# RWKV-7 time mixing on one core: up projections over the whole array, and two groups of per-head sums issued as one

## The chip, the core and the metric

The kernel runs on one core of a Trainium2 chip. Five compute queues matter here: TensorE (PE in the profile; its weight loads are PEld), VectorE (DVE), ScalarE (ACT), GpSimd (POOL), and SyncE (SP), which issues nearly all transfers. The metric is the device time of one execution, in microseconds (us).

## What is computed

One layer: RMS norm, RWKV-7 time mixing with a gate, output projection, residual. SEQ is 2048 and D_MODEL 1024: 16 heads of 64. The part that the change touches, from the reference:

```python
w_lo = jnp.tanh(x_w @ w_in[:, c[4]:c[5]])
a_lo = x_a @ w_in[:, c[5]:c[6]]
w_raw = (w0 + w_lo @ w_up).astype(f32)
log_decay = -jnp.exp(-jax.nn.softplus(-w_raw) - 0.5)
a = jax.nn.sigmoid((a0 + a_lo @ a_up).astype(f32))
...
kk = heads(k * k_k)
kk = kk / jnp.maximum(jnp.sqrt(jnp.sum(kk * kk, axis=-1, keepdims=True)), 1e-12)
...
y = y + jnp.sum(r_h * k_h * r_k.astype(f32), axis=-1, keepdims=True) * v_h
```

`w_up` and `a_up` take 64 low-rank values of a token to 1024 channels: these are the up projections. The sum of `kk * kk` over a head's 64 channels is the sum of squares; the sum of `r * k * r_k` over them is the bonus.

## The kernel before

**Stages.** First (to about 487 us) come the low-rank, value and gate projections of all tokens. Then the tokens go in eight blocks of 256 (NB of TB): for blocks 0 to 6 a function `step(b, p)` runs for p = 0 to 7, one pair of heads each, with 128 channels on the partitions (about 505 to 1054 us). The last block's steps are interleaved with the first chunks of the recurrence, which then runs to the end beside the output projection.

**Numbers in two parts.** A projection's operands are split into a high part and a low part, and a product is three matmuls: high by high, high by low, low by high. A projection of a pair is 24 matmuls of 128x128 by 128x256. The up projections are split otherwise: `up` (L785) holds the weights of both, [:, 0] for the decay and [:, 1] for a, with the high part in one half of the 128 rows and the low part in the other. `split_lo` (L773) makes `lo`, in which the high part of the 64 low-rank values stands twice, in both halves, in [:, 0] and [:, 1]; their low part stands in one half of [:, 2] for the decay and in the other for a. `chain_a` (L789) then issues two matmuls over all 128 rows (L801), and two over 64 rows for the low part (L803). The result `wa` goes to ScalarE (th, ta).

**A step.** `step(b, p)` does four things: r projection of its pair (`rps`, L851), k projection of a pair of the next block (`kps`, L545, begun at the step's start and copied and squared by ScalarE within it: k and sq), products of the pair (`mps`, L887, masked into `mo` by VectorE; `tps`, transposes, L872), and the up projection and decays of the pair after (`chain_a`). `rb` (L829) spreads the factors of the keys' norms over the rows.

**Sums.** `sums` (L712) takes the sums over heads of two pairs at once, by a matmul with a 128x32 matrix of ones and zeros (`hsel`). Each pair has its own 32 of the 128 columns of the array, given by `tile_position`, so a tile of PSUM has the sums of eight pairs in four column tiles of two. The sums of squares of the next block go to `ssp` (from sq), in steps 0, 2, 4 and 6, behind the transposes. The bonuses of this block go to `bnp` (from u, which VectorE makes from the r projection and k): in steps 2, 4 and 6 those of pairs p - 2 and p - 1, behind the masked products; the last two pairs come in step 0 of the next block by `bn_save` (L757), ahead of the up projection. `save` (L718) copies a finished tile to SBUF: `bnc`, `ssc`.

**What sets the order.** The instructions of TensorE, VectorE, ScalarE and GpSimd run in the order in which the code issues them (L1040, a manual schedule). A scheduler places the transfers in SyncE's queue. Each engine works through its queue in order: whatever waits holds all that stands behind it.

**Buffers.** `up` has two buffers, so the weights of a pair are loaded two steps ahead (`load_up(p + 2)`).

Of the kernel before, what the change touches and what calls it, by code (L numbers as in the profile page):

```python
# [39 lines left out]
def rwkv7_kernel(ctx, tc, a, T):  # L40
# [48 lines left out]
    # W_out's rows in the place of two blocks' mixes, once those are used  # L89
# [9 lines left out]
    def rsqrt(pool, out, x, shape, nm):  # L99
        # x in SBUF, positive and normal; out may not alias x  # L100
        y = pool.tile(shape, F32, name=nm + "y", tag="rq", bufs=3)
        t = pool.tile(shape, F32, name=nm + "t", tag="rq", bufs=3)
        h = pool.tile(shape, F32, name=nm + "h", tag="rq", bufs=3)
        ts(y.bitcast(I32), x.bitcast(I32), -0.5, 1597463007.0, mul, add)
        ts(h, x, -0.5, None, mul)
        for it in range(3):
            tt(t, y, y, mul)
            tt(t, t, h, mul)
            stt(y if it < 2 else out, t, 1.5, y, add, mul)
# [14 lines left out]
    def load_w(src, nm, stage, eng=lambda i: None):  # L124
        # steps that load a weight's rows, the row blocks in turn, and the access to its parts
# [24 lines left out]
    def load_wc(src, nm, stage):  # L150
        # the same by column blocks
# [25 lines left out]
    def load_mix(k, mix, b, pool=False, n=NCT // 2):  # L177
        # a projection's mix of the rows, 0: k, 1: r; the steps that split it
# [16 lines left out]
    def gate(b, i, ps, pool, tag="go", bufs=2):  # L195
        # twice silu of the gate's columns i, to DRAM
        go = pool.tile([P, TB], F32, name=f"go{b}_{i}", tag=tag, bufs=bufs)
        act(go, ps, AF.Tanh, scale=0.5)
        stt(go, go, 1.0, ps, add, mul)
        nc.sync.dma_start(g_d[b][:, i], go)  # L200
# [4 lines left out]
    # of half h: partitions of the K|V and of the B|U parts; columns of the A and of the R part  # L205
# [6 lines left out]
    def load_c(ch):  # L212
        # the chunk's [A|R] on the other half's rows, M on its own; token-major [K|B]
# [28 lines left out]
    def decay(ch):  # L242
        # diagonal blocks beside the token-major [K|B]: the chunk's decay of the state
# [59 lines left out]
    def chunk(ch, state, fill):  # L303
        # the recurrence's step, the second wave's end of the chunk before within it
# [28 lines left out]
    def fill(n):  # L333
        # n of the output projection's matmuls between the recurrence's small ones
# [9 lines left out]
    def tail(t):  # L344
        # norm, bonus, gate and output of chunks 4t to 4t + 3, in steps
# [145 lines left out]
    def inversion(g, z, tmp):  # L491
        # z: strict parts, rows (h, chunk, pair); their unit triangular inverses go into M
# [16 lines left out]
    with ExitStack() as p0:  # L509
# [37 lines left out]
        with ExitStack() as pa:  # L547
# [25 lines left out]
            # low rank weights of a token's own and of the token before's normed row  # L573
# [9 lines left out]
            def split_up():  # L583
                # the up projections' weights in high and low parts, stacked to contract at once
# [75 lines left out]
        with ExitStack() as pb:  # L660
# [18 lines left out]
            nc.sync.dma_start(hsel.rearrange("p i c -> p (i c)"), a["hsel"])  # L679
            cb = sm.tile([P, 1], F32, name="cb")  # L680
# [5 lines left out]
            def product(nm, b, p, **k):  # L686
                # a pair's part of what goes to DRAM; in the last block two pairs share a tile and a transfer
                return pairs[nm](p)[:, :, p % 2] if b == NB - 1 else kp.tile([P, NC, 64], F32, name=f"{nm}{b}{p}", **k)

            def store(dst, x, nm, b, p, rows):  # L690
                # dst: rows by chunk by pair
# [32 lines left out]
            def tokenmajor(c, bank):  # L724
                # [P = (j, i, h; 32), TB] sums to token-major [P, 2, (h, i, j)]
# [47 lines left out]
            def split_lo(b, raw):  # L773
                # high parts twice, beside the low ones: the up projections contract both parts of their weights at once
                x = sm.tile([P, 3, TB], F32R, name=f"lo{b}", tag="lo")
                for i in range(2):
                    nc.scalar.copy(x[half(i), i], raw[half(i)])
                for i in range(2):
                    tt(x[half(i), 2], raw[half(i)], x[half(i), i].bitcast(F32), sub)
                    nc.scalar.copy(x[half(1 - i), i], raw[half(i)])  # L780
# [3 lines left out]
            def load_up(p):  # L784
                up = sm.tile([P, 2, P], F32R, name=f"up{p}", tag="up", bufs=2)  # L785
# [3 lines left out]
            def chain_a(b, p):  # L789
# [12 lines left out]
                for j in range(2):  # L802
                    nc.tensor.matmul(wup[j], up[half(j), j], x[half(j), 2], start=False, stop=True)  # L803
                load_up(p + 2)
# [39 lines left out]
            def r_proj(b, p, ps):  # L844
                # the projection's matmuls in two halves
# [19 lines left out]
            def prod_t():  # L865
                # token-major [K|B], decayed to the chunk's end
# [11 lines left out]
            def prod_m():  # L878
                # masked M = [K|B]' [R|A], its strict part to the inversion
# [16 lines left out]
            def preload():  # L896
                # into the freed rows of W_k: the first chunks' operands
# [21 lines left out]
            def step(b, p):  # L919
                # the block's pair p: projections, products, the next block's K; the pair after's decays run ahead  # L920
# [43 lines left out]
                if first and b > 0:  # L964
                    bn_save(b - 1)
# [27 lines left out]
                if p % 2 == 0 and p:  # L993
                    sums(st["bn", b], us, b, p - 2)
# [16 lines left out]
                if p % 2 == 0:  # L1011
                    sums(st["ss", b + 1], sqs, b + 1, p)
                    if p == 6:
                        st["ssc"] = save(st["ss", b + 1], b + 1, "ss")
# [3 lines left out]
            def first_k():  # L1018
                # the first block's K, beside the loads of W_r
# [20 lines left out]
            with tc.manual_schedule(engines=MANUAL):  # L1040
                mixes = deque(load_mix(0, mixb, 1, True))
                load_up(0)
                load_up(1)
# [6 lines left out]
                # the last block, the first chunks' recurrence between its matmuls  # L1050
# [10 lines left out]
                def last():  # L1061
                    # the last block's steps between the parts of the chunks' recurrence
# [60 lines left out]
                def wo_load(p):  # L1123
                    # rows p of W_out into the place of its low part
# [54 lines left out]
    with ExitStack() as p1:  # L1179
# [19 lines left out]
        def background(us):  # L1199
            # elementwise work worth us of the vector engine  # L1200
# [111 lines left out]
```

## Time and profile before

| | |
|---|---|
| Runs | 1656.64, 1653.35, 1651.27 us; median 1653.35 |
| The profiled execution | 1656.64 us, span 1656.3 |
| TensorE busy | 1549.2 us, 94% |
| VectorE busy | 1179.6 us, 71% |
| ScalarE busy | 932.4 us, 56% |
| GpSimd busy | 573.1 us, 35% |

Busy shares are means over stages that have different limits. The chain that ended last goes back from the last instruction to what released each step. The rows in order of time show, for one engine, when an instruction started, how long it lasted, and in brackets how long the engine had been idle before and on what it had waited. Matmuls overlap: one that is given 0.28 us follows its neighbour after about 0.12, so times are best read from start to start. A granted clock of 1.00 is TensorE's 2.4 GHz, 0.50 is 1.2 GHz.

### The profile page before, as it was taken

How to read it: one execution, taken by the hardware profiler on the slowest of the kernel's cores; microseconds unless marked ns; L12 is line 12 of the kernel's file. 1: busy time of each engine (PE TensorE's matmuls, PEld its weight loads, DVE VectorE, ACT ScalarE, POOL GpSimd, SP SyncE). 2: the span in 40 equal slices, each digit the busy share in tenths (PEclk: the TensorE clock that was granted, in tenths of full speed). 3: DMA queues.
4: the chain of work that ended last, by engine and by line, in shares of the span. 5: the costliest groups of instructions: out<-in, count | busy, mean ns of one | idle time of the engine just before them, and what ended most of it. 6: DMA issues, size and time to landing. Idle time of an engine off the chain costs nothing.

```text
span 1656.3 us, 46156 instructions
## 1 busy us (share of the span) xinstructions
PE 1549.2 (94%) x17776; PEld 1311.4 (79%) x17776; DVE 1179.6 (71%) x2592; ACT 932.4 (56%) x2378; POOL 573.1 (35%) x911
## 2 busy tenths in 40 slices
PE   3799999999999999989898989899999999999998
PEld 2589889998798887878787878787677777777776
DVE  7976776667656679897988888857646755765454
ACT  5653332233356455445445454588888778877771
POOL 4500000000002334333334343554556555565541
PEclk9899999999999999999999999999999999999999
DMA  5773433334563565656565657787877677667652
GB/s 183 223 259 125 141 124 106 128 125 155 156 215 111 131 136 134 130 152 139 149 151 144 146 145 150 186 223 222 208 202 197 179 189 201 175 167 206 176 126 86
DMA packets 445740, 269.15 MB, mean 163 GB/s; under 512 B 302768, under 2 KB 386096, under 8 KB 445520
## 3 DMA queue, kind: packets, MB, share of 16 engines
q1 hardware_dynamic: 444176, 261.67, 58.9%
q10 hardware_dynamic: 1344, 4.52, 0.9%
q8 instruction: 141, 2.31, 0.6%
q14 instruction: 79, 0.65, 0.1%
HBM read 158.74 MB, written 111.54 MB: 163 GB/s over the span
## 4 chain that ended last, share of the span: by engine, by line
PE 54%; DVE 20%; issue 6%; DMA 6%; ACT 5%; POOL 3%; SPq 0%; DVEq 0%; POOLq 0%; ACTq 0%
PE ops L465 11%; PE gps L545 10%; PE vps L545 5%; PE kps L545 4%; PE ybank L257 4%; PE rps L851 4%; PE ybank L293 3%; DVE th L809 3%; PE dp L282 3%; PE ubank L269 3%; DVE z L51 2%; DVE tm L51 2%; PE mps L887 2%; DVE bk L51 1%; PE lps L607 1%
## 5 line engine op out<-in xcount | busy, mean ns | idle before, releaser
L545 PE MATMUL gps<-mixbh,wgh 128*128 128x256 f32 x512 | 146.9, 287 | 5.0 <-ACT vo L640 5.0
L247 POOL TENSOR_TENSOR dk<-consts,misc 64x512 f32<-64x512 f32 x128 | 144.3, 1127 | 9.3
L545 PE MATMUL gps<-mixbl,wgh 128*128 128x256 f32 x512 | 146.7, 286 | 0.0
L545 PE MATMUL gps<-mixbh,wgl 128*128 128x256 f32 x512 | 146.7, 286 | 0.0
L545 PE MATMUL kps<-mixbl,wkh 128*128 128x256 f32 x448 | 130.7, 292 | 14.8 <-DVE mixbl L186 14.8
L851 PE MATMUL rps<-mixah,wrh 128*128 128x256 f32 x448 | 132.8, 296 | 2.1 <-ACT sq L60 2.1
L545 PE MATMUL kps<-mixbh,wkh 128*128 128x256 f32 x448 | 134.2, 300 | 0.2 <-DVE u L48 0.2
L545 PE MATMUL kps<-mixbh,wkl 128*128 128x256 f32 x448 | 129.8, 290 | 0.0
L851 PE MATMUL rps<-mixal,wrh 128*128 128x256 f32 x448 | 127.2, 284 | 0.0
L851 PE MATMUL rps<-mixah,wrl 128*128 128x256 f32 x448 | 127.1, 284 | 0.0
L60 ACT ACTIVATE th<-wa,dprm 128x256 f32<-128x256 f32 x64 | 30.4, 475 | 169.4 <-PE wa L803 93.9
L841 POOL TENSOR_TENSOR ra<-th,e 128x256 f32<-128x256 f32 x56 | 47.8, 854 | 211.6 <-DVE th L48 207.6
L97 POOL TENSOR_TENSOR upl<-ups,uph 128x512 fp32r<-128x512 f32 x2 | 2.6, 1287 | 336.3 <-DMA up_d<-uph 333.0
L222 POOL MEMSET x<- 32x512 f32 x128 | 66.4, 519 | 145.4 <-PE ybank L293 137.3
L545 PE MATMUL vps<-wvh,mixah 128*128 128x512 f32 x256 | 106.3, 415 | 5.8 <-ACT mixah L96 4.5
L262 ACT COPY misc<-ybank 32x256 f32<-32x256 f32 x220 | 79.9, 363 | 55.7 <-PE ybank L257 52.0
L465 PE MATMUL ops<-woh,oh 128*128 128x512 f32 x256 | 109.5, 428 | 1.6 <-ACT oh L444 1.6
L465 PE MATMUL ops<-woh,ol 128*128 128x512 f32 x256 | 110.4, 431 | 0.0
L465 PE MATMUL ops<-wol,oh 128*128 128x512 f32 x256 | 107.2, 419 | 0.0
L545 PEld LDWEIGHTS gps<-mixbh,wgh 128*128 128x128 f32 x512 | 99.9, 195 | 5.4 <-ACT vo L640 5.4
L545 PE MATMUL vps<-wvl,mixah 128*128 128x512 f32 x256 | 103.5, 404 | 0.0
L545 PEld LDWEIGHTS kps<-mixbl,wkh 128*128 128x128 f32 x448 | 89.1, 199 | 16.0 <-DVE mixbl L186 16.0
(326 smaller groups left out, 4909.4 us busy)
## 6 DMA issues: line engine op xcount, KB each, us to landing
stat<-sm_d SPq DMA_DIRECT2D x64, 512.0 KB, 5.0
dk<-bt_d SPq DMA_DIRECT2D x128, 128.0 KB, 4.6
sm_d<-ra SPq DMA_DIRECT2D x112, 128.0 KB, 3.2
sm_d<-mo SPq DMA_DIRECT2D x112, 128.0 KB, 2.7
bt_d<-bo SPq DMA_DIRECT2D x56, 256.0 KB, 3.3
up<-up_d SPq DMA_DIRECT2D x66, 128.0 KB, 2.7
xn<-x SPq DMA_DIRECT2D x32, 256.0 KB, 4.4
mkr_d<-mok SPq DMA_DIRECT2D x64, 128.0 KB, 1.9
```

The lines of the kernel that those rows point to most:

```text
L51: return nc.vector.tensor_tensor(out=out, in0=in0, in1=in1, op=op)
L222: nc.gpsimd.memset(x[bu(h), h], 0.0)
L247: nc.gpsimd.tensor_tensor(out=dk[ch % len(dk)][H, h], in0=ident[H, None, H].broadcast_to([64, NP, N]), in1=pls[g][H, c, :, None].broadcast ...
L257: nc.tensor.matmul(y[half(h), p], st[:, h, 4 * w + p], x[:, h, 4 * w + p], start=(p == 0), stop=(p == 3), tile_position=(0, 64 * h))
L262: nc.scalar.copy(gs[bu(h)], y[kv(h)])
L269: nc.tensor.matmul(bank[2][rb, p], st[rb, h, 4 * w + p, ca], gs[rb, p], start=True, stop=True, tile_position=(rb.start, rb.start))
L282: nc.tensor.matmul(dp[half(1 - h), p], d[:, h, 4 * w + p], x[:, h, 4 * w + p], start=True, stop=True, tile_position=(0, 64 * (1 - h)))
L293: nc.tensor.matmul(bank[w][rb, ch % 2, p], st[rb, h, 4 * w + p, cr], x[rb, h, 4 * w + p], start=False, stop=(p == 3), skip_group_check=Tru ...
L465: nc.tensor.matmul(ps, l[:, ct], r(ct, ns), start=(ct == 0 and k == 0), stop=(ct == NCT - 1 and k == 2))
L545: nc.tensor.matmul(ps, x, y, start=first, stop=last)
L809: nc.vector.tensor_tensor_scan(th, rmask.rearrange("p c l -> p (c l)"), th, 0.0, mul, add)
L851: nc.tensor.matmul(ps, x, y, start=first, stop=last)
```

## The change

In `split_lo` the low parts get two slots, [:, 2] and [:, 3], in a tile `lo_x` that lives through all blocks; the other half of each slot is cleared once by GpSimd ahead of the loop. The two matmuls of the low part then contract all 128 rows: half of them are zeros. `up` has one buffer, and a pair's weights are loaded one step ahead. In the even steps the sums of squares move from behind the transposes to behind the masked products, beside the bonuses, so that four matmuls on four column tiles follow each other; in step 0 `bn_save` moves there too, from ahead of the up projection. The copies `bnc` and `ssc` move along with their sums.

```diff
+            lo_x = sm.tile([P, 4, TB], F32R, name="lo_x")
+            for i in range(2):
+                nc.gpsimd.memset(lo_x[half(1 - i), 2 + i].bitcast(F32), 0.0)
...
             def split_lo(b, raw):
-                x = sm.tile([P, 3, TB], F32R, name=f"lo{b}", tag="lo")
+                x = lo_x
...
-                    tt(x[half(i), 2], raw[half(i)], x[half(i), i].bitcast(F32), sub)
+                    tt(x[half(i), 2 + i], raw[half(i)], x[half(i), i].bitcast(F32), sub)
...
             def load_up(p):
-                up = sm.tile([P, 2, P], F32R, name=f"up{p}", tag="up", bufs=2)
+                up = sm.tile([P, 2, P], F32R, name=f"up{p}", tag="up")
...
                 for j in range(2):
-                    nc.tensor.matmul(wup[j], up[half(j), j], x[half(j), 2], start=False, stop=True)
-                load_up(p + 2)
+                    nc.tensor.matmul(wup[j], up[:, j], x[:, 2 + j], start=False, stop=True)
+                load_up(p + 1)
...
-                if first and b > 0:
-                    bn_save(b - 1)
...
                 if not final:
                     prod_m()
-                if p % 2 == 0 and p:
-                    sums(st["bn", b], us, b, p - 2)
+                if p % 2 == 0:
+
+                    sums(st["ss", b + 1], sqs, b + 1, p)
+                    if p:
+                        sums(st["bn", b], us, b, p - 2)
+                    elif b > 0:
+                        bn_save(b - 1)
+                    if p == 6:
+                        st["ssc"] = save(st["ss", b + 1], b + 1, "ss")
...
                 if not final:
                     prod_t()
-                if p % 2 == 0:
-                    sums(st["ss", b + 1], sqs, b + 1, p)
-                    if p == 6:
-                        st["ssc"] = save(st["ss", b + 1], b + 1, "ss")
```

The lines of the changed kernel stand four further down: L801, L803, L715 and L887 become L805, L807, L719 and L891.

TensorE's queue in step 2 of block 2, before: wa is the up projection's result, mps the masked products, bnp and ssp the sums, rps and kps the projections, tps the transposes.

```order
L803 MATMUL wa_8537<-lo_7988,up_8273 128x256
L803 MATMUL wa_23_8538<-lo_7988,up_8273 128x256
L887 MATMUL mps_8562<-ra_8404,bk_8405 64x64 x16
L715 MATMUL bnp_8536<-u_8120,hsel 32x256
L715 MATMUL bnp_8536<-u_8285,hsel 32x256
L851 MATMUL rps_8588<-mixah,wrh_5741 128x256
...
L872 MATMUL tps_8625<-consts,bk_8405 128x128 x4
L715 MATMUL ssp_8172<-sq_8423,hsel 32x256
L715 MATMUL ssp_8172<-sq_8550,hsel 32x256
L545 MATMUL kps_8651<-mixbh,wkh_5247 128x256
```

The same place after the change:

```order
L807 MATMUL wa_8535<-lo_x,up_8414 128x256
L807 MATMUL wa_23_8536<-lo_x,up_8414 128x256
L891 MATMUL mps_8560<-ra_8402,bk_8403 64x64 x16
L719 MATMUL ssp_8170<-sq_8421,hsel 32x256
L719 MATMUL ssp_8170<-sq_8548,hsel 32x256
L719 MATMUL bnp_8534<-u_8118,hsel 32x256
L719 MATMUL bnp_8534<-u_8279,hsel 32x256
L855 MATMUL rps_8588<-mixah,wrh_5742 128x256
...
L876 MATMUL tps_8625<-consts,bk_8403 128x128 x4
L545 MATMUL kps_8649<-mixbh,wkh_5247 128x256
```

The two sums of squares stand ahead of the r projection's 24 matmuls instead of behind them, and the transposes are followed by the k projection at once.

TensorE's queue in step 0 of block 2, before:

```order
L829 MATMUL rb_8250<-rsT,selb 128x256
L715 MATMUL bnp_7375<-u_7816,hsel 32x256
L715 MATMUL bnp_7375<-u_7953,hsel 32x256
L801 MATMUL wa_8267<-lo_7988,up_7941 128x256
L801 MATMUL wa_21_8268<-lo_7988,up_7941 128x256
...
L887 MATMUL mps_8292<-ra_8043,bk_8044 64x64 x16
L851 MATMUL rps_8316<-mixah,wrh_5655 128x256
...
L715 MATMUL ssp_8172<-sq_8261,hsel 32x256
L715 MATMUL ssp_8172<-sq_8280,hsel 32x256
```

And after:

```order
L833 MATMUL rb_8248<-rsT,selb 128x256
L805 MATMUL wa_8261<-lo_x,up_8075 128x256
L805 MATMUL wa_21_8262<-lo_x,up_8075 128x256
...
L891 MATMUL mps_8286<-ra_8041,bk_8042 64x64 x16
L719 MATMUL ssp_8170<-sq_8259,hsel 32x256
L719 MATMUL ssp_8170<-sq_8274,hsel 32x256
L719 MATMUL bnp_7374<-u_7815,hsel 32x256
L719 MATMUL bnp_7374<-u_7952,hsel 32x256
L855 MATMUL rps_8316<-mixah,wrh_5656 128x256
```

Here the up projection comes earlier by the two bonus sums, and all four sums now stand between the masked products and the r projection.

## Rows read from the trace of the kernel before

**Rows 1.** The page: share of the chain that ended last, by engine.

```profile
PE 54%; DVE 20%; issue 6%; DMA 6%; ACT 5%; POOL 3%; SPq 0%; DVEq 0%; POOLq 0%; ACTq 0%
```

**Rows 2.** Timeline, TensorE, step 2 of block 2: start, duration, instruction, count, [idle before].

```profile
689.92 0.48 PE L801 MATMUL wa<-lo,up 128*128 128x256 f32 x2
690.33 0.38 PE L803 MATMUL wa<-lo,up 64*128 64x256 f32 x2
...
691.72 0.62 PE L715 MATMUL bnp<-u,hsel 128*32 128x256 f32 x4
692.28 0.38 PE L851 MATMUL rps<-mixah,wrh 128*128 128x256 f32 x1
...
695.25 0.60 PE L872 MATMUL tps<-consts,bk 128*128 128x128 f32 x4
695.78 0.63 PE L715 MATMUL ssp<-sq,hsel 128*32 128x256 f32 x4
696.34 0.39 PE L545 MATMUL kps<-mixbh,wkh 128*128 128x256 f32 x1
```

**Rows 3.** Timeline, ScalarE, the same step.

```profile
690.75 0.47 ACT L60 ACTIVATE th<-wa,dprm 128x256 f32<-128x256 f32 x1 [3.17 <-PE wa L803]
...
691.92 0.48 ACT L60 ACTIVATE sq<-kps,prm 128x256 f32<-128x256 f32 x1
```

**Rows 4.** Timeline, TensorE, end of step 3 and step 4 of block 2.

```profile
704.49 0.63 PE L872 MATMUL tps<-consts,bk 128*128 128x128 f32 x4 [0.21 <-DVE mo L51]
704.88 0.36 PE L545 MATMUL kps<-mixbh,wkh 128*128 128x256 f32 x1
...
707.88 0.48 PE L801 MATMUL wa<-lo,up 128*128 128x256 f32 x2
...
713.83 0.63 PE L872 MATMUL tps<-consts,bk 128*128 128x128 f32 x4 [0.46 <-DVE mo L51]
...
714.94 0.39 PE L545 MATMUL kps<-mixbh,wkh 128*128 128x256 f32 x1
```

**Rows 5.** Timeline, ScalarE, step 4 of block 2.

```profile
709.16 0.47 ACT L60 ACTIVATE th<-wa,dprm 128x256 f32<-128x256 f32 x1 [3.41 <-DVE z L51]
...
710.69 0.48 ACT L60 ACTIVATE sq<-kps,prm 128x256 f32<-128x256 f32 x1
```

**Rows 6.** Timeline, TensorE, step 0 of block 2: first bonus sums, then k projection.

```profile
671.63 0.63 PE L715 MATMUL bnp<-u,hsel 128*32 128x256 f32 x4
...
678.56 0.39 PE L545 MATMUL kps<-mixbh,wkh 128*128 128x256 f32 x1
```

**Rows 7.** Timeline, ScalarE, the same step.

```profile
674.36 0.37 ACT L707 COPY k<-kps 128x256 f32<-128x256 f32 x1 [0.25 <-POOL u L838]
674.63 0.48 ACT L60 ACTIVATE sq<-kps,prm 128x256 f32<-128x256 f32 x1
```

**Rows 8.** Timelines: step 6 of block 2 (TensorE, ScalarE); step 0 of block 0.

```profile
728.53 0.63 PE L715 MATMUL bnp<-u,hsel 128*32 128x256 f32 x4
...
729.96 0.48 ACT L60 ACTIVATE sq<-kps,prm 128x256 f32<-128x256 f32 x1
...
521.30 0.48 ACT L60 ACTIVATE sq<-kps,prm 128x256 f32<-128x256 f32 x1
```

**Rows 9.** Timeline, TensorE, two long waits: block 0 step 0, block 3 step 7.

```profile
519.22 0.39 PE L851 MATMUL rps<-mixah,wrh 128*128 128x256 f32 x1 [2.13 <-ACT sq L60]
...
822.70 0.38 PE L545 MATMUL kps<-mixbl,wkh 128*128 128x256 f32 x1 [2.56 <-DVE mixbl L186]
```

**Rows 10.** Stretches: length; PE, PEld, DVE, ACT, POOL busy (records); clock; DMA; GB/s.

```profile
520.55:523.96 3.41, 3.41 (x18) 3.00 (x18) 2.19 (x4) 2.33 (x6) 1.65 (x5) 0.50 0.02 5
523.96:527.37 3.41, 3.41 (x30) 3.02 (x26) 0.55 (x2) 0.00 (x0) 0.38 (x1) 1.00 0.34 77
820.93:824.33 3.40, 1.63 (x13) 1.63 (x14) 3.19 (x10) 0.40 (x1) 0.48 (x2) 1.00 0.93 294
```

**Rows 11.** Waits between 510 and 1075 us: total, times, longest.

```profile
DVE tm L51 <- DMA z<-sm_d: 3.0, 3, 1.4
```

More of the change, by code (lines that the diff above doesn't have):

```diff
@@ L1042, in rwkv7_kernel @@
                 load_up(0)
-                load_up(1)
                 wr, st["wr"] = load_wc(a["w_r"], "wr", stage)
```

## The prediction

> **What bounds the kernel now.** I read the chain that ended last first: TensorE carries 54% of it and VectorE 20% [rows 1]. So a microsecond of TensorE is worth about half of one on average, and the average says little about one stage. The change works in the middle phase, where blocks 0 to 6 go through eight steps each, and a little in the last block. So the next view is single steps in order of time. I call a step by its pair, 0 to 7, as the code does.
>
> Three kinds of step come out. In step 2 TensorE goes without a gap: up projection (L801, L803), masked products, bonus sums, 24 matmuls of the r projection, transposes, sums of squares, next k projection [rows 2]. TensorE sets the pace, and a block of sums costs there what stands between its start and the next row: bonus sums 691.72 to 692.28, sums of squares 695.78 to 696.34, 0.56 us each. Steps 1 and 2 and nearly all of block 0 are like this. In step 4 the transposes wait 0.46 us for VectorE's mo [rows 4]; steps 3, 5 and 6 wait likewise, so VectorE paces them. Step 7 hangs on the split of the next mix: TensorE waits 2.56 us for mixbl in the middle of its k projection [rows 9].
>
> **What is removed, added and moved.** The number of instructions on TensorE does not change.
>
> (1) Low parts over the whole array. L803's two matmuls use half of the rows each. From the first L801 to L803 is 0.41 us [rows 2], two starts; the r projection's like neighbours start 2.97 / 24 = 0.12 apart (692.28 to 695.25), which would make 0.24, so up to 0.17 goes. The two L803, which can lie side by side, come at most 0.12 apart: +0.12. So −0.17 to +0.12 a step; I take −0.05, between the two, since only a part of the 0.41 need be the change of shape. It counts in some 10 odd steps that TensorE paces: −0.5 us. The Trainium skill, TensorEngine Tiling (Array Packing), Key Properties, says that changing the tiling mode drains TensorE; the 0.41 agrees with that, and by this rule alone the term would lie at the −0.17 end, 10 × −0.17 = −1.7.
>
> (2) Two blocks of sums become one. The 27 even steps that had both (block 0: 2, 4, 6; blocks 1 to 6: 0, 2, 4, 6) now issue four matmuls on four column tiles. If all four run beside each other, one block of 0.56 goes: 27 × 0.56 = 15.1 us of TensorE time gross. If the pairs follow each other, it is 1.12 and nothing goes. I take the first, because the 0.56 for two is nearer to one matmul's time than to two in turn with their weights. The Trainium skill, TensorE: Matmul & The Clock Gate, Part 3, says that column tiles run concurrently at some 4 ns more each; no row of before shows four.
>
> (3) The new wait. The sums of squares read sq of the pair whose k projection ended just before this step, and ScalarE makes it within this step: two th operations, the copy of k, then sq. Before, sq had the whole r projection to be made in; now TensorE comes to it right after the masked products. Queued behind the waiting matmul are the bonus sums, the r projection, the transposes and the next k projection. From the start S of the four sums, the k projection starts at S + 0.56 + 2.97 + 0.39 = S + 3.92 (0.39 is transposes to k projection where no sums stand between, 704.49 to 704.88 [rows 4]).
> - Step 2: sq ends at 691.92 + 0.48 = 692.40; its chain begins with th, which waited for wa [rows 3], and wa comes 0.1 to 0.2 earlier by (1). S is about 692.25 and the k projection starts at 696.17 (up to 696.32) against 696.34 [rows 2]. TensorE waits about 0.6 at the sums, and of the 0.56 saved 0 to 0.2 is left. I take 0.15; with the seven steps 2 and steps 4 and 6 of block 0, which run alike: 9 × −0.15 = −1.3 us.
> - Step 4 of blocks 1 to 6: th is late, having waited for VectorE's z. sq ends at 710.69 + 0.48 = 711.17 [rows 5], S = 711.22, the k projection starts at 715.14 against 714.94 [rows 4]: 6 × 0.2 = +1.2. TensorE is at the sums at 707.88 + 1.75 = 709.63 (1.75 as from L801 to the bonus sums in [rows 2]) and idles 1.6 us.
> - Step 0 of blocks 1 to 6: the bonus sums ahead of L801 go, so L801 starts at 671.63, 0.56 earlier; but the copy of k waits for GpSimd's u (until 674.36), which nothing here makes earlier [rows 6, 7]. sq ends at 674.63 + 0.48 = 675.11, S = 675.16, the k projection starts at 679.08 against 678.56: 6 × 0.5 = +3.0, with an idle of 1.7 us.
> - Step 6: sq ends at 729.96 + 0.48 = 730.44, the sums' place is at 728.53 [rows 8]: an idle of 1.9 us. The shift (some 0.7 at the step's end) falls on step 7's products, which wait for VectorE's ra; I cost it at nothing. Without that cover it is 6 × 0.7 = +4.
> - Block 0, step 0: the r projection started at 519.22 [rows 9]; now it stands behind sums whose sq ends at 521.30 + 0.48 = 521.78 [rows 8]. It starts at 521.83 + 0.56 = 522.39, 3.2 later, less the 0.56 of the sums that stood behind it: +2.6. A stretch at half clock that slowed it before, 18 records against 30 in 3.41 us, so 12 × 0.12 = 1.4 us [rows 10], may fall into the new wait: +1.2 to +2.6; I take +2.0.
>
> (4) What absorbs. VectorE waits in three places for the load of z, up to 1.4 us each [rows 11]; a transfer sets these times, so what TensorE loses ahead of them is not lost. That takes back about half of step 0's loss in the later blocks: −1.5 (0 to −2).
>
> (5) Clock. A half clock follows some waits of TensorE and not others: 0.50 from 520.55 after one of 2.13 us, but 1.00 around one of 2.56 in 820.93 to 824.33 [rows 9, 10]. The 12 new waits of 1.7 to 1.9 us (steps 0 and 6) are a little shorter, so a few may be followed by a half clock, at 1.4 us a stretch where TensorE paces, half of that where VectorE does. I take +1.0 (0 to 6 × 1.4 + 6 × 0.7 = +12.6). The Trainium skill, TensorE: Matmul & The Clock Gate, Part 1, says that the throttled clock is the default and activity releases it; the fall after 2.13 us agrees.
>
> (6) The rest. `up` with one buffer is loaded one step ahead instead of two; steps 2 and 3 take 707.88 − 689.92 = 17.96 us [rows 2, 4], so a step is some 9 long, and the longest wait for a load here is 1.4 [rows 11]: 0, bound +1.4, in the last block. Two GpSimd clears ahead of the loop and the two ScalarE copies (bnc later, ssc earlier): 0, bounds −0.5 to +1, hidden beside step 7's wait.
>
> Sum: −0.5 − 1.3 + 1.2 + 3.0 + 2.0 − 1.5 + 1.0 = +3.9 us. The profiled execution took 1656.64 us, 0.2% above the median of 1653.35, so the sum needs no scaling: 1653.35 + 3.9 = 1657.2, and I say 1657. About 0.3% (5 us) is what a measurement here can tell from no change; this lies within it.
>
> **Rivals.**
> - The saved block arrives. If sq comes 0.5 us or more earlier than I place it (an order or a release on ScalarE that I misread), the 9 steps like step 2 and the 6 steps 0 give their 0.56: 15 × 0.56 = 8.4, with (1) some 9 us, 1644. For it: sq is only 0.6 late in step 2. Against it: [rows 5, 7] name VectorE and GpSimd as what holds ScalarE, and neither gets faster.
> - Slower, by the clock. If 9 of the 12 new waits of steps 0 and 6 are followed by a stretch at 0.50, this costs about 9 in place of the 1.0: 1665; with all, 1669. It passes the bound of 0.3% from two falls in steps 0 on. For it: 2.13 sufficed; against it: the 2.56 that did not [rows 9, 10].
> - Four column tiles run as two pairs in turn. Then each merged block takes 0.56 more behind the wait: 21 steps outside step 6, 12 us, less about a third that VectorE and the loads hide: +8, 1665. Against it: two already cost little more than one.
> - The single buffer of `up`, or the copies, cost more than I see: +1 to +2, 1658 to 1659.
>
> **How the numbers follow.** My forecast 0.45 (its own range 1653 to 1662); the gain arrives 0.24; the clock 0.20; tiles in turn 0.06; the buffer 0.05. Faster by over 0.3% is the second case but for its weakest part: 0.22. Slower takes 0.13 of the forecast, whose upper part passes 1658.3, 0.16 of the clock case, 0.04 and 0.02 of the others: 0.35. The rest, 0.43, is within 0.3%. The range is 1646 to 1668: down to most of the full gain, up to the clock case and the tiles in turn.
>
> **What would show it.** In the profile after: TensorE waits for sq at the sums, about 0.6 us in step 2, 1.6 in step 4, 1.7 in step 0, 1.9 in step 6; the four sums take about 0.6 us from their first start to the r projection; the k projection of step 0 starts 4.0 after sq's end. It is wrong if these waits are missing or under 0.3 us, if the four sums take 1.1, or if the granted clock shows many more stretches of 0.50.

## The result, and the profile after

The changed kernel takes 1662.91 us in the median of four runs (1661.37 to 1670.47), the kernel before beside it 1653.91. The ratio is 1.0069, 95% interval 1.0047 to 1.009. Run again on another chip beside before, it gave 1663.38 against 1656.64, ratio 1.0037 (1.0019 to 1.0054). So the change makes the kernel slower by about half a per cent, 6 to 11 us in the two comparisons. That is inside the predicted range (1646 to 1668), but past the 1657 that was forecast as likeliest and past the 0.3% within which it was to stay.

One run of 2793.11 us, of the first of the two shifted kernels below, is left out of that kernel's median.

The profiled execution took 1670.47 us, 0.45% above its median, and is the slowest of its four; the second profile (1667.82) is the slowest of its ten. A step's difference can be read from them, but their sum is larger than what the medians differ by. The page after, busy shares and the chain that ended last, which answer to [rows 1]:

```profile
PE 1540.3 (92%) x17776; PEld 1316.9 (79%) x17776; DVE 1176.0 (70%) x2592; ACT 930.9 (56%) x2378; POOL 573.8 (34%) x913
...
PE 55%; DVE 19%; ACT 6%; DMA 6%; issue 6%; POOL 3%; SPq 1%; DVEq 0%; POOLq 0%; ACTq 0%
```

TensorE has 9 us less work, and the span is longer: it waits more. The waits in the middle phase say for what (total us, times, longest):

```profile
PE ssp L719 <- ACT sq L60: 28.4, 22, 2.2
ACT u L60 <- PE bnp L719: 12.1, 27, 0.7
PE tps L876 <- DVE mo L51: 7.5, 12, 1.3
DVE mo L51 <- DMA sm_d<-mo: 4.5, 2, 2.7
...
PE wa L805 <- DMA up<-up_d: 0.6, 1, 0.6
```

The first line is the wait that the prediction placed there. The second and the fourth were not in it. The last, a wait for the single buffer of `up`, stood in it only as a bound. Step 4 of block 2 on TensorE, which answers to [rows 4] (start, duration, instruction, count, [idle before]):

```profile
714.36 0.48 PE L805 MATMUL wa<-lo_x,up 128*128 128x256 f32 x2
714.68 0.41 PE L807 MATMUL wa<-lo_x,up 128*128 128x256 f32 x2
...
716.10 0.62 PE L719 MATMUL ssp<-sq,hsel 128*32 128x256 f32 x2
717.71 0.40 PE L719 MATMUL ssp<-sq,hsel 128*32 128x256 f32 x1 [0.99 <-ACT sq L60]
...
718.27 0.39 PE L855 MATMUL rps<-mixah,wrh 128*128 128x256 f32 x1
...
721.60 0.37 PE L545 MATMUL kps<-mixbh,wkh 128*128 128x256 f32 x1
```

Of the two sums of squares, the pair whose sq is old runs at once (716.10); the other waits until 717.71. From there to the r projection is 0.56 us, to the k projection 3.89; the prediction had S + 0.56 and S + 3.92. The idle that the profile shows (0.99) is shorter than the 1.6 that was forecast, because one matmul already fills 0.62 of it: the delay of all that stands behind is the same. In step 2 this goes so far that the profile shows no idle at all, where the prediction named a wait of about 0.6 us as its sign; the older pair's matmul fills it, and the block of sums takes 1.28 us from its first start to the r projection, against 0.56 [rows 2]:

```profile
696.98 1.02 PE L719 MATMUL ssp<-sq,hsel 128*32 128x256 f32 x3
...
698.26 0.39 PE L855 MATMUL rps<-mixah,wrh 128*128 128x256 f32 x1
```

Step 0 of block 2 on TensorE, which answers to [rows 6]:

```profile
676.38 0.48 PE L805 MATMUL wa<-lo_x,up 128*128 128x256 f32 x2
...
680.08 0.40 PE L719 MATMUL ssp<-sq,hsel 128*32 128x256 f32 x1 [1.35 <-ACT sq L60]
...
683.97 0.37 PE L545 MATMUL kps<-mixbh,wkh 128*128 128x256 f32 x1
```

and on ScalarE, which answers to [rows 7]:

```profile
679.27 0.37 ACT L711 COPY k<-kps 128x256 f32<-128x256 f32 x1 [0.68 <-POOL u L842]
679.54 0.48 ACT L60 ACTIVATE sq<-kps,prm 128x256 f32<-128x256 f32 x1
```

sq ends at 680.02, the second sum starts at 680.08, the k projection 3.95 after sq's end. GpSimd's u holds ScalarE as it did before, now 0.68 us instead of 0.25, since the rest comes earlier.

**Where the time went.** Worked out from the starts of the up projection (first L801 or L805 of each step) in the profiled executions, as the sum over blocks of what each kind of step took longer than before, in us. Steps 6 and 7 and the next step 0 stand together, since the bonus sums moved over the border between 7 and 0 and step 7 can take up what step 6 loses.

| steps | change, first profile | change, second | step 0 put back | block 0's step 0 put back |
|---|---|---|---|---|
| 0 of block 0 | +3.4 | +3.1 | 0.0 | −1.5 |
| 1 to 6 of block 0 | 0.0 | 0.0 | 0.0 | 0.0 |
| 6 and 0 of blocks 1 to 6, 7 of blocks 0 to 5 | +3.6 | +2.7 | −0.5 | +0.4 |
| 1 of blocks 1 to 6 | +0.5 | +1.2 | +0.4 | +1.4 |
| 2 and 3 of blocks 1 to 6 | +1.3 | +0.6 | −1.6 | −0.6 |
| 4 and 5 of blocks 1 to 6 | 0.0 | 0.0 | 0.0 | 0.0 |
| 7 of block 6 | +1.6 | +1.9 | +0.7 | +0.7 |

The loss sits in the steps 0 and in what follows from them. The last two columns are experiments, told below. Where TensorE's clock is at half speed for a stretch (a granted clock of 0.50) differs from one profile to the next, and some of these numbers hang on that; the part on why the prediction was right or wrong takes it out.

### The profile page after: what moved, and what is told of

The parts are those of the page before. It is cut to its first block, busy times and chain, and to the rows that moved or that the text cites. A ratio compares the mean times of both kernels' runs of the same rounds, so it can differ in the third digit from the quotient of the medians.

```text
span 1668.7 us, 46137 instructions
## 1 busy us (share of the span) xinstructions
PE 1540.3 (92%) x17776; PEld 1316.9 (79%) x17776; DVE 1176.0 (70%) x2592; ACT 930.9 (56%) x2378; POOL 573.8 (34%) x913
## 4 chain that ended last, share of the span: by engine, by line
PE 55%; DVE 19%; ACT 6%; DMA 6%; issue 6%; POOL 3%; SPq 1%; DVEq 0%; POOLq 0%; ACTq 0%
PE ops L465 11%; PE gps L545 10%; PE rps L855 5%; PE vps L545 5%; PE kps L545 5%; PE ybank L257 4%; PE ybank L293 3%; PE dp L282 3%; PE ubank L269 2%; DVE z L51 2%; DVE tm L51 2%; DVE th L813 2%; PE mps L891 1%; PE lps L607 1%; DVE bk L51 1%
## 5 line engine op out<-in xcount | busy, mean ns | idle before, releaser
L545 PEld LDWEIGHTS gps<-mixbl,wgh 128*128 128x128 f32 x512 | 99.7, 195 | 0.0
```

What stands on the lines that cost most here:

```text
L545: nc.tensor.matmul(ps, x, y, start=first, stop=last)
```

## Experiments

The theory at this point: TensorE's new wait for sq, above all in the steps 0, costs the time. The rivals: the single buffer of `up` and the transfers that moved; the clock; four column tiles that don't run beside each other; ScalarE's new wait for the bonus sums.

**The two halves of the change.** First the low parts over the whole array and the single buffer of `up`, with all sums at their old places; then the sums merged, with everything else as before. The first, against the kernel before:

```diff
-                    nc.tensor.matmul(wup[j], up[half(j), j], x[half(j), 2], start=False, stop=True)
-                load_up(p + 2)
+                    nc.tensor.matmul(wup[j], up[:, j], x[:, 2 + j], start=False, stop=True)
+                load_up(p + 1)
```

> The low parts over the whole array and the single buffer of `up` alone; all sums stay where they were before. Theory (the cost comes from TensorE's new waits for sq): no such wait here, so -0.5 to -1.5 us against before, about 1653, within 0.3%. Rival (the single buffer of `up` and the transfers that it moves cost the time): +4 us or more, 1658 to 1662, with longer waits of VectorE for z or of TensorE for `up`.

Measured: 1656.04 against 1654.75, ratio 1.0001 (0.9984 to 1.0018). The up projection in step 2 of block 2:

```profile
688.39 0.48 PE L804 MATMUL wa<-lo_x,up 128*128 128x256 f32 x2
688.72 0.41 PE L806 MATMUL wa<-lo_x,up 128*128 128x256 f32 x2
689.05 1.15 PE L890 MATMUL mps<-ra,bk 64*64 64x64 f32 x32
```

From the first matmul to the masked products it is 0.66 us, 0.72 before: −0.06 a step, where −0.05 was taken. From the first pair to the second it is 0.33 instead of 0.41. So zeros in half of the rows cost nothing, and hardly anything is won. The rival of the single buffer falls: in the whole time it shows nothing, within 3 us. In single steps it does show: in this run's profile TensorE waits 2.4 us for `up`, in two places. In the change it waits 0.6 us at the end of step 1 of block 3, which is the +0.5 of the table's row for step 1; in the second profile 0.9 us, in blocks 3 and 4. With the sums merged alone, and two buffers, that row is 0.0. The second, against the kernel before:

```diff
-                if first and b > 0:
-                    bn_save(b - 1)
...
-                if p % 2 == 0 and p:
-                    sums(st["bn", b], us, b, p - 2)
+                if p % 2 == 0:
+                    sums(st["ss", b + 1], sqs, b + 1, p)
+                    if p:
+                        sums(st["bn", b], us, b, p - 2)
+                    elif b > 0:
+                        bn_save(b - 1)
```

> The merged sums alone: the low parts stay on 64 rows, `up` keeps two buffers. Theory: nearly the whole loss of the change, +8 to +10 us, about 1662 to 1664, with waits for sq of 0.6 us in step 2, 1.6 in step 4, 1.7 or more in step 0 and 1.9 in step 6. Rival (single buffer): not more than +4 us, 1654 to 1658.

Measured: 1665.63 against 1654.75, ratio 1.0056 (1.0036 to 1.0076). The merged sums alone carry the whole loss.

**The place without the wait.** The sums of squares at their new place, but of a constant in place of sq in blocks 1 to 7, which leaves the keys' norms out.

```diff
+            flat = consts[:, 191:192].broadcast_to([P, TB])
...
+                    for x in (p, p + 1):
+                        sqs[b + 1, x] = flat
                     sums(st["ss", b + 1], sqs, b + 1, p)
```

> The change, but in blocks 1 to 7 the sums of squares are taken of a column of ones in place of sq, which leaves the keys' norms out: four matmuls at the same place, with nothing of ScalarE to wait for. Theory: the block is saved and the waits are gone, 1644 to 1650; the stretches at half clock in steps 0 of blocks 1 and 4 go too. Rival (the wait is not the cause, but the place, the tiles or `up`): 1658 to 1663, as the change.

Measured: 1651.31 against 1654.75, ratio 0.9972 (0.9956 to 0.9989), 0.7% to 1% less than the change. So the wait is the cause, not the place. Yet the gain is 2 to 7 us, less than the 8 to 10 of the saved blocks. Its waits in the middle phase:

```profile
PE tps L877 <- DVE mo L51: 20.9, 26, 1.6
DVE tm L51 <- DMA z<-sm_d: 8.7, 5, 2.5
...
PE wa L806 <- DMA up<-up_d: 7.3, 6, 3.1
```

Before, z took 3.0 [rows 11], the load of `up` does not appear, and mo took 13.1 us:

```profile
PE tps L872 <- DVE mo L51: 13.1, 29, 1.1
```

What TensorE gains, VectorE, the load of z and the single buffer of `up` take back in part. How much each of them takes was not tested.

**The sums later.** The four sums together behind the transposes, where sq is long ready: a way to save the block without the wait, it seemed.

```diff
                 if not final:
                     prod_t()
...
+                if p % 2 == 0:
+                    sums(st["ss", b + 1], sqs, b + 1, p)
+                    if p:
+                        sums(st["bn", b], us, b, p - 2)
```

> The change with the four sums moved behind the transposes, where the sums of squares stood before: sq is ready there, so the four matmuls stay one block and the wait for sq goes. Theory: TensorE gets the saved block in the steps that it paces, 15 x 0.56 = 8 us less than before, some of it hidden: 1645 to 1650. Rival (four column tiles run as two pairs in turn): the block takes 1.1 us in place of 0.6, 1652 to 1654. Rival (clock or `up`): as slow as the change, 1660 or more.

Measured: 1712.47, ratio 1.0334 (1.031 to 1.0359): none of the cases. The waits name it:

```profile
ACT u L60 <- PE bnp L719: 82.6, 25, 3.6
```

u has three buffers. It goes through three engines: ScalarE makes its first form, GpSimd multiplies that by k, and VectorE by the r projection, all in one buffer. So the reading is this: a sum of bonuses that comes late keeps the u of two pairs, the step's own is the third, and ScalarE, which begins the next pair's u early in the step, waits for the sum. The same wait, 12.1 us in 27 places, stands in the profile of the change. It is a second new wait that the prediction missed. Two runs test it: the change with the bonus sums ahead of the sums of squares, which frees u before the wait for sq; and late sums with a fourth u buffer (its space from a single buffer of `up`). The first, against the change:

```diff
+                    if p:
+                        sums(st["bn", b], us, b, p - 2)
+                    elif b > 0:
+                        bn_save(b - 1)
                     sums(st["ss", b + 1], sqs, b + 1, p)
-                    if p:
-                        sums(st["bn", b], us, b, p - 2)
-                    elif b > 0:
-                        bn_save(b - 1)
```

> The change with the bonus sums ahead of the sums of squares within the merged block. TensorE's end of the block stays at sq's end + 0.6, but ScalarE's u no longer waits for the bonus sums behind the waiting matmul (12.1 us in 27 places after the change). Theory that this second wait, which the prediction did not have, is part of the excess: 2 to 5 us less than the change, 1657 to 1660. Rival (only TensorE's wait for sq counts): as the change, 1661 to 1664.

Measured: 1665.91 against 1656.64, ratio 1.0057 (1.0039 to 1.0074); the change itself, on the same chip, 1.0037 (1.0019 to 1.0054). The wait of u is gone from the waits, and the time is no shorter: those 12 us lie beside TensorE's own wait and cost nothing. The theory that they are part of the excess falls. The second, from the kernel before with the late sums:

```diff
-                u = tp.tile([P, TB], F32, name=f"u{b}{p}", tag="u", bufs=3)
+                u = tp.tile([P, TB], F32, name=f"u{b}{p}", tag="u", bufs=4)
```

> From the kernel before: one buffer for `up`, and in the space that this frees a fourth buffer for u; the four sums together behind the transposes, the low parts on 64 rows as before. With three buffers ScalarE's u waited 82.6 us for the late bonus sums. Theory: with four that wait is gone, sq is long ready, and TensorE saves one block of sums: 4 to 8 us less than before, 1646 to 1650. Rival (late sums hold something else, or four tiles do not save a block): 1653 or more.

Measured: 1660.17 against 1656.64, ratio 1.0015 (0.9997 to 1.0032). No u wait is left, and step 2 takes 8.88 us instead of 9.43 in blocks 0 to 2, so the block is saved; but the time is not less:

```profile
PE tps L872 <- DVE mo L51: 28.3, 27, 2.1
DVE tm L51 <- DMA z<-sm_d: 8.8, 5, 2.5
```

The gain turns up as longer waits for mo and for z, as in the run without sq. The late sums also stand between the transposes and the k projection in step 0, which takes about 10.2 to 10.8 us.

**Step 0.** The change again beside before, and with its step 0 put back to the old order.

> The changed kernel once more, beside the kernel before on the same chip, for a second profile and a narrower interval. Every theory: 0.5% to 0.9% slower than before, 1661 to 1664; the stretches at half clock may lie in other steps than in the first profile.

Measured: as in the section on the result, 1.0037; its profile is the second column of the table.

```diff
-                if p % 2 == 0:
+                if p % 2 == 0 and p:
                     sums(st["ss", b + 1], sqs, b + 1, p)
...
+                if first and b > 0:
+                    bn_save(b - 1)
...
+                if first:
+                    sums(st["ss", b + 1], sqs, b + 1, p)
```

> The change with step 0 put back: the two bonus sums ahead of the up projection, the sums of squares behind the r projection; steps 2, 4 and 6 stay merged. Theory (step 0, with block 0's first step and the half clock behind its waits, carries most of the loss): 6 to 9 us less than the change, 1653 to 1657. Rival (steps 4 and 6 or the transfers carry it): not more than 3 us less, 1659 to 1662.

Measured: 1655.66 against 1656.64, ratio 0.9988 (0.9971 to 1.0005). With the waits of steps 4 and 6 still there (12 of the 13 places of this line; in step 2 there is no idle), the whole loss is gone: it hung on the steps 0 and on what follows from them.

```profile
PE ssp L719 <- ACT sq L60: 15.7, 13, 1.4
```

Then only block 0's step 0 put back.

```diff
-                    sums(st["ss", b + 1], sqs, b + 1, p)
+                    if b or p:
+                        sums(st["ss", b + 1], sqs, b + 1, p)
...
+                if first and b == 0:
+                    sums(st["ss", 1], sqs, 1, 0)
```

> The change, with the sums of squares of block 0's step 0 alone put back behind the r projection; all other steps as changed. Theory (there the r projection stood 3.1 to 3.4 us longer behind a wait of TensorE that ended at half clock): 3 us less than the change, 1659 to 1661, and step 0 of block 0 back at 11.0 us. Rival (what is saved at the start is given back at later transfers): 1662 to 1664.

Measured: 1658.57 against 1654.41, ratio 1.0019 (1.0004 to 1.0033). The change beside its own before had 1.0069 and 1.0037, so this is 0.2% to 0.5% less, 3 to 8 us; against the second of the two the intervals overlap, and the size is uncertain. In the profile the step takes 9.55 us, not the 11.0 that was expected, against 14.42 in the change. But 1.5 us of that is not the order's doing: the run with all steps 0 put back has the same order in this step and the same wait, and takes 11.02 there, as the kernel before does (11.03); the clock is 1.00 in the one and 0.50 in the other. The r projection's first matmul and the stretch of the clock, with block 0's step 0 put back and then with all steps 0 put back (a stretch: length; PE, PEld, DVE, ACT, POOL busy and records; clock; DMA; GB/s):

```profile
518.49 0.38 PE L855 MATMUL rps<-mixah,wrh 128*128 128x256 f32 x1 [2.19 <-ACT sq L60]
518.49:521.90 3.41, 3.41 (x28) 3.07 (x28) 2.64 (x5) 2.39 (x6) 2.47 (x5) 1.00 0.02 5
...
520.24 0.46 PE L855 MATMUL rps<-mixah,wrh 128*128 128x256 f32 x1 [2.17 <-ACT sq L60]
520.42:523.83 3.41, 3.41 (x17) 3.41 (x18) 2.45 (x5) 2.40 (x7) 2.29 (x4) 0.50 0.02 5
```

TensorE in block 0's step 0 of the change (the two sums of squares, each with its wait, and what follows), and then three stretches:

```profile
520.28 0.62 PE L719 MATMUL ssp<-sq,hsel 128*32 128x256 f32 x2 [2.18 <-ACT sq L60]
522.88 1.06 PE L719 MATMUL ssp<-sq,hsel 128*32 128x256 f32 x2 [1.97 <-ACT sq L60]
...
523.87 0.58 PE L855 MATMUL rps<-mixah,wrh 128*128 128x256 f32 x1
...
528.88 0.29 PE L545 MATMUL kps<-mixbh,wkh 128*128 128x256 f32 x1
```

```profile
521.74:525.15 3.41, 2.27 (x8) 1.46 (x9) 1.91 (x3) 2.33 (x6) 1.64 (x5) 0.50 0.00 0
525.16:528.57 3.41, 3.41 (x18) 3.41 (x18) 0.00 (x0) 0.00 (x0) 0.22 (x1) 0.51 0.02 5
600.20:603.61 3.41, 3.41 (x18) 3.41 (x17) 1.44 (x3) 1.29 (x4) 0.89 (x2) 0.50 0.21 47
```

The clock falls to 0.50 within the second wait and stays there for two stretches, and the second one covers most of the r projection: it takes 5.0 us (523.87 to 528.88). At full clock it takes 3.0; before, with one stretch at 0.50 [rows 10], it took 4.4, from 519.22 [rows 9] to the sums behind it:

```profile
523.59 0.79 PE L715 MATMUL ssp<-sq,hsel 128*32 128x256 f32 x4
```

All four profiles with two waits in this step (the change twice, the merged sums alone, the bonus sums first) have two stretches there, and the step takes 14.1 to 14.6 us.

In block 1's step 0 (600.20) the clock falls once more, and that step takes 12.7 us; so it does in the second profile of the change and with the bonus sums first. With block 0's step 0 put back, no fall comes there, and it takes 11.2. The link is not a fixed one: with the merged sums alone, block 0's step 0 is as long (14.1), and block 1's takes 11.2 without a fall. Nor is the fall in block 1 one more than before. There one came a little earlier, in step 7 of block 0:

```profile
585.40:588.81 3.41, 3.41 (x19) 3.35 (x18) 2.87 (x6) 1.63 (x5) 0.93 (x2) 0.50 0.42 149
```

**Saving the block without the wait.** If the sums of step p take the squares of pairs p − 1 and p instead of p and p + 1, sq is ready. Each pair's squares go one column tile further, so that the four tiles still differ. Against the kernel before:

```diff
+            def sums_k(b, *ps):
+                for p in ps:
+                    i, j = divmod((p + 1) % NP, 4)
+                    nc.tensor.matmul(st["ss", b][32 * j : 32 * j + 32, 0], hsel[:, i], sqs.pop((b, p)), start=(p < 4),
+                                     stop=(p > 3), tile_position=(0, 32 * j))
...
+                if p % 2 == 0:
+                    sums_k(b + 1, *((p - 1, p) if p else (0,)))
...
+                if p == 6:
+                    sums_k(b + 1, 7)
```

> From the kernel before, the four sums together behind the masked products as in the change, but of pairs whose sq is ready: step p sums the squares of pairs p - 1 and p (step 0 of pair 0 alone; pair 7 behind the transposes of step 6), each pair's squares one column tile further, so that the four tiles still differ. Theory: no wait for sq, one block of sums less in steps 0, 2 and 4; as the run without real sq, 0.2% to 0.4% less than before, 1649 to 1653. ScalarE's sq waits instead for the sums, some 0.4 us, which costs little. Rival (VectorE's wait for z takes the gain back, as it did with late sums and four u buffers): 1654 to 1660.

Measured: 1654.22 against 1654.41, ratio 0.9997 (0.9982 to 1.0012): on the side of the rival. In its profile steps 6, 7 and 0 (the table's third row) are 5.6 us shorter than before, and steps 2 and 3 are 6.5 longer. VectorE's wait for z is 7.0 us, and TensorE waits longer for mo:

```profile
PE tps L879 <- DVE mo L51: 25.0, 28, 2.4
```

> The same with a third buffer for sq, so that ScalarE doesn't wait for the sums either; its space comes from `up`, which has one buffer. Theory: as the kernel with two sq buffers or up to 2 us less, 1648 to 1653. Rival (the single buffer of `up`, for which TensorE waited in other runs, costs more than the wait for sq): 1 to 3 us more than the one with two sq buffers.

Measured: 1651.28 against 1654.41, ratio 0.9987 (0.9975 to 0.9999): just faster than before, by 0.1%, and 0.5% or more faster than the change. This one shows the four tiles without a wait between them, step 2 of block 2:

```profile
687.21 0.41 PE L722 MATMUL ssp<-sq,hsel 128*32 128x256 f32 x2
687.22 0.41 PE L715 MATMUL bnp<-u,hsel 128*32 128x256 f32 x2
687.45 0.39 PE L722 MATMUL ssp<-sq,hsel 128*32 128x256 f32 x2
687.46 0.39 PE L715 MATMUL bnp<-u,hsel 128*32 128x256 f32 x2
687.78 0.38 PE L858 MATMUL rps<-mixah,wrh 128*128 128x256 f32 x1
```

Four matmuls take 0.57 us from the first start to the r projection, two took 0.56 [rows 2]: the rival of the tiles in turn falls. But the blocks saved in steps 0, 2 and 4 are worth 20 x 0.56 = 11 us gross (step 6 saves none, since pair 7 keeps a place of its own), and some 2 (0.2 to 4) arrive. The waits of this run show where others stay:

```profile
DVE tm L51 <- DMA z<-sm_d: 9.2, 5, 2.4
...
PE wa L808 <- DMA up<-up_d: 4.5, 6, 1.8
```

VectorE waits for z 9.2 us instead of 3.0, and TensorE waits for the single buffer of `up`. As in the kernel with two sq buffers, most of what steps 6, 7 and 0 gain in its profile (6.3 us) is lost again in steps 2 and 3 (5.6).

## Why the prediction was right or wrong

**Right: the mechanism of step (3).** sq is not ready, and everything behind it on TensorE waits. In the steps looked at, the terms of S were right to 0.03 us (3.89 against 3.92), four tiles take one block's time, and the loss is in the steps 0, as the sum said (+3.0 and +2.0 of its +3.9). Term (1), −0.05 a step, measured −0.06; of the 0.17 at the bound no more came. For the later steps 0, compare only places with the clock alike. Before, steps 6, 7 and the next 0 take 33.9 to 34.1 us where a stretch at 0.50 falls in step 7 (blocks 1, 2, 4 and 5), and 33.3 where none does (block 3). In the two profiles of the change they take 34.3 to 34.7 and 33.7 to 34.0. So the change costs about 0.5 us a block either way, some 2.8 us over six blocks, where the prediction had +3.0. With all steps 0 put back they take 34.0 to 34.1 and 33.5, so nearly all of it is the wait in step 0.

**Wrong in size: block 0's step 0.** The prediction took +2.0 with an upper bound of 2.6, because a stretch at half clock "may fall into the new wait". It does, but a second stretch follows, and the r projection runs in it: +3.1 to +3.4. The bound missed the case in which the longer wait brings more half clock instead of hiding it: from the second sum to the r projection it is 0.99 us instead of 0.56, and the r projection takes 5.0 us instead of 4.4. The Trainium skill, TensorE: Matmul & The Clock Gate, Part 1, has the throttled clock as the default; two stretches at 0.50 around two waits of about 2 us agree with that.

**About right in sum, wrong in place: the clock, step (5).** The prediction expected a few falls more, in steps 0 and 6, and took +1.0. Between 516 and 1054 us the kernel before has six stretches at 0.50, and so has the change, in either profile; what differs is where they lie. Before, one lies in block 0's step 0 and five in steps 7 (blocks 0, 1, 2, 4 and 5). In the change two lie in block 0's step 0, and of the other four two in steps 0 and two in steps 7 in the first profile, one and three in the second.

A stretch in step 7 costs 0.7 us by the numbers above (in block 0 about 0.9: 31.95 us before, 31.09 in the run with all steps 0 put back, where none falls). One in step 0 costs 1.4 to 1.5: 35.2 where it falls in block 4's step 0 against 33.8 without, and 33.0 where it falls in block 1's against 31.5 with block 0's step 0 put back. By this estimate that makes 3.7 us in all before, and 4.3 and 3.6 in the change, so outside block 0's step 0 the clock costs about 0 to 0.6 us more. With the second stretch in block 0's step 0, some 1 us (the 0.4 and 0.6 above), it is 1.0 to 1.6, near the +1.0. The mean granted clock of the runs that stood side by side on one chip hardly differs, 0.9839 for the change (10 runs) and 0.9845 for the kernel before (31 runs). The rival "slower, by the clock" wanted nine new falls, and they did not come. Its counterexample was a bad guide as well: the 2.56 us wait in block 3 [rows 9, 10] is the only one of six such waits in steps 7 of before around which the clock stays at 1.00.

**Too large: the gain in step 2, −1.3.** The nine steps that were to gain came out 0.0 and 0.1 us shorter in all. Most steps 2 are 0.1 shorter, but step 6 of block 0, which was counted as one of them, is 0.47 longer (8.24 against 7.77).

**Outweighed: what absorbs, step (4).** The prediction took −1.5 for VectorE's waits for z. They did shrink, from 3.0 us to 0.9 and 1.7. But a new wait of VectorE came, for the stores of mo: 4.5 and 3.9 us, in step 2 of blocks 2 and 3. In block 3 it stands in the place of a wait for z, and steps 2 and 3 together are hardly longer than before; in block 2 they lose 1.2 us. VectorE's wait in block 2:

```profile
700.57 0.69 DVE L51 TENSOR_TENSOR mo<-mps,consts 128x512 f32<-128x512 f32 x1 [1.77 <-DMA sm_d<-mo]
```

and SyncE's queue shows why; the loads and stores of that place, before and then after the change:

```profile
686.87 1.25 SPq L696 DMA_DIRECT2D sm_d<-mo  x2
688.23 1.91 SPq L495 DMA_DIRECT2D z<-sm_d  x2
...
692.57 2.13 SPq L495 DMA_DIRECT2D z<-sm_d  x2
694.75 2.49 SPq L700 DMA_DIRECT2D sm_d<-mo  x2
```

In block 2 the scheduler has put the load of z ahead of the stores of mo, where before the stores stood first. The stores start later, and the next mo has no buffer. With all steps 0 or only block 0's put back, SyncE's order in block 2 is again that of before, and this wait is not there. So 1.2 us of what these two runs gain comes by way of the transfers. The prediction did not price this move.

**Right to cost at nothing: step 6. Wrong: step 4's +1.2.** Step 6 alone is 2.3 us longer over the blocks (9.29 to 9.64 each), and step 7 takes it back, as the cover said: with all steps 0 put back, steps 6, 7 and 0 together are 0.5 us shorter than before, and with the clock alike hardly longer. Step 4's +1.2 did not come, since step 5 is shorter by as much (10.09 and 8.77 became 10.23 and 8.61): VectorE sets the sum of the two (in step 5 the transposes wait for mo before and after, 0.46 and 0.36 us). There the prediction left out a cover that it had named itself, VectorE's pace.

**Small, but not nothing: the single buffer of `up`, step (6).** Its bound of +1.4 was placed in the last block. TensorE's waits of 0.6 and 0.9 us came in blocks 3 and 4, and step 1 is +0.5 and +1.2 in the table.

**Missed: ScalarE's wait for the bonus sums**, 12.1 us. It costs nothing, as the run with the bonus sums first shows; it would have decided the case had the sums stood later (+58 us).

**Open.** Step 7 of block 6, on the way to the last block, is 1.6 to 1.9 us longer in the two profiles of the change, but 0.4 shorter with the merged sums alone. It goes with the clock: the mean granted clock of this step is 0.90 before, 0.83 and 0.68 in the change, 0.91 with the merged sums alone, and 0.82 in the two runs with steps put back, where the step is 0.7 longer. Why the clock falls more there was not tested; no run was aimed at it.

Taken together, in us, for the first and the second profile: block 0's step 0, 3.4 and 3.1; steps 6, 7 and 0 of the later blocks, 3.6 and 2.7 (some 2.8 of it the wait, the rest where the clock falls); the single buffer of `up` in step 1, 0.5 and 1.2; steps 2 and 3, 1.3 and 0.6, with the transfers' 1.2 in block 2; the open step, 1.6 and 1.9. That makes 10.4 and 9.5, where the middle phase is 10.3 and 9.6 longer in the two profiles. The medians differ by 7 to 9 us, and the runs of one kernel spread over 9 us and more. So the excess over the forecast of +3.9 is accounted for in these profiles; that each share has the same size in an ordinary run is not shown.

## What to carry to other kernels

Moving work earlier in an engine's queue is free only if its operand is ready there: look up the end of the operand's producer in the trace first, and count all that is queued behind. Joining small matmuls on separate column tiles does save TensorE's time (four for the price of two), though here only 0.1% of the kernel's came of it. So choose the operands that are ready, here by a shift of one pair, rather than the place. Check how long the moved reader holds its inputs: with too few buffers, a later sum stops the engine that makes the next input. Before a difference is put down to the clock, count the stretches at half clock in both profiles, and compare steps in which they lie alike.

## What was not expected of the hardware

A sum at the new place needs no more time with four column tiles than with two, 0.57 against 0.56 us, so the second pair is free. Two waits of about 2 us with a single matmul between them were followed by two stretches at a granted clock of 0.50 (521.74 to 528.57), and the step took 14.1 to 14.6 us in the four profiles that have them. A single wait of that size at the same place was followed by one stretch before (2.13 us, the step takes 11.03) and with all steps 0 put back (2.17, 11.02), but by none with block 0's step 0 put back (2.19, 9.55). The same order and the same wait can go either way, so a step's time in a single profile is uncertain by 1.5 us there.
